# Priorities, smaller pieces and one step per visit in a kernel of four mixers

## The chip, the core and the metric

The kernel runs on one core of a Trainium2 chip. The time is that of the device for one execution, in microseconds. TensorE (PE) multiplies, VectorE (DVE), ScalarE (ACT) and GpSimd (POOL) do the rest, and SyncE (SP) issues the DMAs. Each engine works through a queue of its own that is written out when the program is built.

## The reference

One layer with four sequence mixers side by side, in fp32: x is 2048 tokens of 1024.

```python
h = rmsnorm(x, pre_norm_w)
p = h @ w_in                                  # 1024 -> 3992 columns
y_gdn  = gated_deltanet(p_gdn)                # conv, l2norm, chunks of 64, triangular solve, state 64x64 per head
y_rwkv = rwkv7(p_rwkv)                        # token shift, decay, delta rule with a learned rate, group norm, bonus
y_sc   = bg * causal_conv(cg * xv) * silu(z)  # short convolution
y_gla  = gla(p_gla)                           # gated linear attention, key width 32, value width 64
out = x + rmsnorm(concat(y_gdn, y_rwkv, y_sc, y_gla) @ w_out)
```

Each of the three recurrent mixers has 4 heads of 64 values. In gla, with q, k, v cut in chunks of 64 tokens and b the running sum of the log decay: `attn = tril((q e^b)(k e^-b)^T)`, `o = attn v + (q e^b) S`, `S = S e^(b_last) + (k e^(b_last - b))^T v`.

## The kernel before

The sequence is worked in four blocks of 512 tokens (`BL`), a block in four tiles of 128 (`TT`), a tile in two chunks of 64. Projections multiply in single-pass fp32 with each operand split in a high and a low part: three products per pair, so one projection tile of 128 columns is 24 matmuls of 512 tokens into one PSUM bank of two (`pp`). Weights are loaded per block (`load_parts`, in halves of 256 KB of columns; the split form comes from DRAM from the second block on).

The program is emitted by generators that are woven together (`weave`). The last one, the projections and then the output projection, is the main thread with number 99. Above it run the recurrences: `chains` (priority 0: state updates of gdn, rwkv and gla, tile by tile), `inverses` (1: the triangular inverses, two tiles of four heads at a time, by doubling in half precision), `prepare` (2: gates, norms, decays and matrices of both mixers), `put` and `rwkv_bonus` (3), the norms of the next block (4). A thread yields either an event that it waits for or a time (`LAT`) after which it may go on; the planner's clock `t` runs by the matmuls emitted. Whenever some thread is ready and the main thread has had `BEAT` = 1.5 of that clock, the ready threads are run, again and again until none is ready; then the main thread has the word again.

The order of emission is the priority of each instruction. `tc.high_priority(offset=n)` moves what is emitted in it n places ahead. The framework that builds the program lays out each engine's queue from these priorities and its own model of when an instruction can start. The evacuations of the projection banks have an offset of 400, as the weight splits have; everything in the mixers has none.

What the change touches: `inverse` (L591 to L658: copies to the block diagonal Bb and Yb, L613 W, L618 X, L620 the transpose Y), `gdn_chain` (L1005 to L1030, gu, the state Sg), `add_state` (L1037), `rwkv_chain` (L1056 ru, L1064 UV, L1079 the copy that ends a tile), `rwkv_prep` (two halves `pr` of 128 channels; scan L893, products L903 to L911), `gla_proj`, `proj_v`, `gla_prep`, and `gla` (L1286 to L1314). In gla's projection v is made by token: the normed input is the stationary operand and 256 weight columns move, into both banks at once, four quarters of the weights after another. One tile of `lv` then holds two tiles of tokens with 256 channels each. q, k and z are made by channel.

Of the kernel before, what the change touches and what calls it, by code (L numbers as in the profile page):

```python
# [19 lines left out]
P = 128  # L20
# [25 lines left out]
CST = {"ident": 0, "dlt": 128, "cum": 256, "msi": 384, "rst": 640, "bones": 640 + BL}  # L46
NCST = 640 + BL


def make_consts():  # L50
    c = np.zeros((P, NCST + P), np.float32)
    r = np.arange(P)
    blk = r[:, None] // 64 == r[None, :] // 64
    a, b = r[:, None] % 64, r[None, :] % 64
    c[:, 0:128] = np.eye(P)
    c[:, 128:256] = blk & (a > b)
    c[:, 256:384] = blk & (a <= b)
    j, i = r[:, None] % 64, np.arange(64)[None, :]

    c[:, 384:640] = np.concatenate([i > j, i >= j, i >= j, i > j], 1)  # L60
    c[:, 640:NCST] = np.arange(BL) % 64 > 0
    c[:, NCST:] = blk

    m = [j == i, -((j // 2 == i // 2) & (i % 2 == 1) & (j % 2 == 0)).astype(np.float32)]
    m += [-((j // (2 * s) == i // (2 * s)) & (j % (2 * s) >= s) & (i % (2 * s) < s)).astype(np.float32) for s in LEVELS]
    return c, np.concatenate([x.astype(np.float16) for x in m], 1)


def layout(inp):
# [4 lines left out]
    starts += [GLA0, GLA0 + 128, GLA0 + 512, GLA0 + 640]  # L74
# [5 lines left out]
    wv = w[:, GLA0 + 256:GLA0 + 512].reshape(KT, P, 256).transpose(1, 0, 2).reshape(P, KT * 256)  # L80
# [8 lines left out]
    for nm, key in (("w0", "rwkv_w0"), ("a0", "rwkv_a0"), ("kk", "rwkv_k_k"), ("ka", "rwkv_k_a"), ("rk", "rwkv_r_k"),  # L89
# [13 lines left out]
        "wv": wv,  # L103
# [24 lines left out]
class Ring:  # L128
# [6 lines left out]
    def __call__(self):  # L135
# [15 lines left out]
    "lqk": (BL, 2), "lv": (BL, 2), "lk": (128, 1), "lgz": (2 * BL, 1), "ld": (8, 1), "lg": (BL, 2), "n32": (32, 4), "gs": (TT, 2),  # L151
# [16 lines left out]

BEAT = 1.5
# [4 lines left out]
       "invr": 0.8, "chA": 1.0, "chB": 0.7, "chC": 0.48, "rpre": 5.0, "rchan": 4.5, "gpre": 3.0, "gA": 1.1,  # L174
# [14 lines left out]

class K:  # L190
    def __init__(self, tc, a, out):
        self.tc, self.nc, self.a, self.out = tc, tc.nc, a, out
        self.t, self.left, self.ev, self.threads = 0.0, 0.0, {}, []
# [11 lines left out]
    def thread(self, gen, prio):  # L205
        self.threads.append([prio, 0.0, None, gen])
        self.threads.sort(key=lambda th: th[0])
# [11 lines left out]
    def step(self, th):  # L219

        y = next(th[3], "end")
        if y == "end":
            self.threads.remove(th)
        elif isinstance(y, tuple):
            th[2] = y
        else:
            th[1] = self.t + y

    def weave(self):
# [3 lines left out]
        while self.threads:  # L233
            main = self.threads[-1]
            ready = [th for th in self.threads if th[0] < 99 and self.can(th)]
            if main[0] == 99 and self.can(main) and (not ready or self.t - self.left < BEAT):
                self.step(main)
            elif ready:
                while ready:
                    for th in ready:  # L240
                        self.step(th)
                    ready = [th for th in self.threads if th[0] < 99 and self.can(th)]
                self.left = self.t
            else:
                if not any(self.can(th) for th in self.threads):
                    w = [th[1] for th in self.threads if th[2] is None]
                    assert w, [(th[0], th[2]) for th in self.threads]
                    self.t = max(self.t, min(w))


    def setup(self, ctx):
# [29 lines left out]
        self.rst = g("rst", BL)  # L281
        c16 = c.tile([P, 64 * (2 + len(LEVELS))], F16, name="c16")
# [187 lines left out]
    def load_half(self, blk, wi, i):  # L470
# [10 lines left out]
    def proj(self, blk, groups):  # L481
# [3 lines left out]
        for n, (_, tiles, _) in enumerate(groups):  # L485
            nj = range(len(tiles))
            halves = [(n, j, i) for i in range(4 if tiles[0][0] == "v" else 2) for j in nj]
# [8 lines left out]
        for n, j, i, ks in work:  # L496
# [10 lines left out]
            if first:  # L507
                pss[n, j] = self.pp() if tiles[j][0] != "v" else [self.pp() for _ in range(2)]
# [3 lines left out]
            if tiles[j][0] == "v":  # L512
                yield from self.proj_v(ps, i, pairs)
                if i == 3:
                    with self.tc.high_priority(offset=PRIO):
                        tiles[j][1](ps)
                fin += 1
                continue
# [14 lines left out]
            yield 0.0  # L533

    def proj_v(self, ps, i, pairs):

        for q, (w, h) in enumerate(pairs):
            for k in range(2):
                for t in range(TT):
                    o = 256 * (t % 2)  # L540
                    self.mm(ps[t // 2][:, o:o + 256], h[:, 2 * i + k, t * P:(t + 1) * P], w[:, k, :], start=(i + q + k + t % 2 == 0),
                            stop=(i == 3 and q == 2 and k == 1), skip_group_check=True)
# [37 lines left out]
    def inverse(self, Bh, Bl, n):  # L580
# [9 lines left out]
        for c in range(2):  # L590
            nc.vector.tensor_copy(Bb[hs(c), :, hs(c)], Bh[hs(c)])  # L591
# [6 lines left out]
        nc.vector.tensor_tensor(Y, Bh, m4(self.n1t), ALU.mult)  # L598
        nc.vector.tensor_tensor(Y, Y, I16, ALU.add)
        X = self.R16["X"]()  # L600
        nc.vector.transpose(X, Y)
        def diag():
            Yb = self.Rbd["Yb"]()
            for c in range(2):
                nc.vector.tensor_copy(Yb[hs(c), :, hs(c)], Y[hs(c)])  # L605
# [3 lines left out]
        for lv in range(4):  # L609
# [3 lines left out]
            nc.vector.tensor_tensor(W, v(ps), m4(self.lev[lv]), ALU.mult)  # L613
# [4 lines left out]
            nc.vector.tensor_tensor(X2, v(ps), X, ALU.add)  # L618
            X = X2
            nc.vector.transpose(Y, X)  # L620
# [5 lines left out]
        nc.vector.tensor_tensor(W, v(ps), m4(self.lev[4]), ALU.mult)  # L626
# [8 lines left out]
        nc.vector.tensor_tensor(X2, v(px), X, ALU.add)  # L635
        nc.vector.tensor_tensor(Y, py, Y, ALU.add)
# [3 lines left out]
        nc.vector.tensor_tensor(T, I16, X, ALU.subtract)  # L640
# [8 lines left out]
        nc.vector.tensor_tensor(R, T, v(ps), ALU.subtract)  # L649
# [8 lines left out]
        nc.vector.tensor_tensor(v(Yf), v(ps), Y, ALU.add)  # L658
# [210 lines left out]
    def rwkv_prep(self, blk):  # L869
# [10 lines left out]
        for pr in range(2):  # L880
# [15 lines left out]
            nc.scalar.activation(e[:, :, 1:65], c3(G), AF.Exp)  # L896
            ev = e.rearrange("p (a c) t -> p a c t", c=2)
# [95 lines left out]
    def gdn_chain(self, tt, m, Y):  # L993
# [5 lines left out]
        for cp in range(2):  # L999
# [5 lines left out]
            nc.vector.tensor_tensor(h4(D)[q], h4(pA[:, 0:256])[q], bc(g["ne1"])[q], ALU.mult)  # L1005
            nc.vector.tensor_tensor(D[q], D[q], m["vT"][q], ALU.add)
            nc.vector.tensor_tensor(h4(t)[qn], h4(pA[:, 0:256])[qn], bc(g["e1s"])[qn], ALU.mult)
            n = 8 * cp + 2 * tt
            nc.vector.tensor_tensor(S, S, g["dec"][:, n:n + 2].unsqueeze(2).to_broadcast([P, 2, P]), ALU.mult)
# [5 lines left out]
            for hp in range(2):  # L1015
                nc.scalar.copy(qh(w)[q, :, hp, :], pB[hs(hp), 0:P].rearrange("p (q d) -> p q d", q=2))
# [12 lines left out]
        for cp in range(2):  # L1029
            nc.vector.tensor_tensor(og[hs(cp)], t[hs(1 - cp)], pO[hs(1 - cp), 0:256], ALU.add)  # L1030
        return og

    def add_state(self, S, pC):
        pv = pC[:, 0:P].rearrange("p (q d) -> p q d", q=2)
        for hp in range(2):
            sb = S[hs(hp), :, hs(hp)]
            self.nc.vector.tensor_tensor(sb, sb, pv[hs(hp)], ALU.add)  # L1037

    def rwkv_chain(self, tt, m, Y):
# [11 lines left out]
        for cp in range(2):  # L1051
# [4 lines left out]
            nc.scalar.copy(D[q], pAc[cp][q])  # L1056
            nc.vector.tensor_tensor(S, S, r["dec"][:, :, c:c + 1].to_broadcast([P, 2, P]), ALU.mult)
# [4 lines left out]
            for hp in range(2):  # L1062
                s = slice(4 * tt + hp, 4 * tt + hp + 3, 2)
                nc.vector.tensor_tensor(qh(uv[:, cp, :])[q, :, hp, :], pB[hs(hp), 0:P].rearrange("p (q d) -> p q d", q=2),  # L1064
# [13 lines left out]
        for cp in range(2):  # L1078
            nc.scalar.copy(og[hs(cp)], pAc[cp][hs(1 - cp)])  # L1079
# [156 lines left out]
    def gla_proj(self):  # L1236
# [4 lines left out]
        todo = [(None, ((WT_GLA + i, lambda ps, t=t: nc.scalar.copy(t, ps)),), None) for i, t in enumerate((qf, kf))]  # L1241
# [6 lines left out]
        todo.append((None, ((WT_GLA + 2, z(0)), (WT_GLA + 3, z(1))), "gla"))  # L1248
        return dict(q=qf, k=kf, v=v, gz=gz), todo

    def gla_prep(self):
# [24 lines left out]
    def gla(self, blk, tt):  # L1276
# [8 lines left out]
        at, ke, vt = u1(), self.R["lk"](), L["v"][tt // 2][:, 256 * (tt % 2):256 * (tt % 2) + 256]  # L1285
        nc.vector.tensor_tensor(h4(at), h4(pa[:, 0:256]), self.incl.unsqueeze(1).to_broadcast([P, 4, 64]), ALU.mult)  # L1286
        pt = self.psa()
        self.tr(pt[:, 0:P], L["ed"][:, ts], self.ident)
        nc.scalar.copy(ke, pt[:, 0:P])
# [7 lines left out]
        pC = pa[:, 256:320], pt[:, 128:192]  # L1297
# [4 lines left out]
        for cp in range(2):  # L1302
# [3 lines left out]
            nc.vector.scalar_tensor_tensor(self.Sl, self.Sl, L["dec"][:, c:c + 1], pC[cp], ALU.mult, ALU.add)  # L1306
# [7 lines left out]
        nc.scalar.copy(o, po[:, 0:256])  # L1314
# [145 lines left out]
```

## Time and profile before

| | |
|---|---|
| median of 3 runs | 1378.37 us (1376.46 to 1379.8) |
| the profiled execution | 1379.89 us, its span 1378.1 us |
| PE busy | 1284.7 us, 93%, 10088 matmuls |
| DVE / ACT / POOL busy | 967.7 / 530.2 / 355.5 us (70 / 38 / 26%) |
| granted clock of TensorE, mean | 0.985 |
| DMA | 204.63 MB, mean 148 GB/s |

The span cut in 40 equal slices; a digit is the busy share of a slice in tenths:

```
PE   5989988899999999999999999999998998999997
DVE  5766698869876895778657978888669847743232
```

[...] A wait is put down to the producer that came last.

### The profile page before, as it was taken

The numbers are of one execution on the slowest core, as the hardware profiler recorded it, in microseconds if no ns is written. First come the engines' busy times: TensorE is split into PE (matmuls) and PEld (weight loads), VectorE is DVE, ScalarE is ACT, GpSimd is POOL, SyncE is SP. The second block draws the span as 40 slices with busy tenths as digits, with TensorE's granted clock in tenths as the row PEclk, the third lists the DMA queues.
The fourth block names the chain that finished last, engine by engine and source line by source line (L and its number), as shares of the span: only waits on it lengthen the run. The fifth ranks groups of instructions, "written<-read, shape, count | busy, mean of one in ns | idle before, by whom it ended". The sixth has DMA issues, their size and how long they took to land. (4 is left out here: it accounts for less than half of the span.)

```text
span 1378.1 us, 26007 instructions
## 1 busy us (share of the span) xinstructions
PE 1284.7 (93%) x10088; PEld 982.1 (71%) x10088; DVE 967.7 (70%) x2194; ACT 530.2 (38%) x1167; POOL 355.5 (26%) x437
## 2 busy tenths in 40 slices
PE   5989988899999999999999999999998998999997
PEld 3767766767667767767777677776776776677886
DVE  5766698869876895778657977888669847743232
ACT  4663454336242431425423432453224325133221
POOL 5554444201221021101301210203111135233321
PEclk9999999999999999999999999999999999999999
DMA  8776554544244424453543335432444363233442
GB/s 283 263 258 231 206 177 146 177 152 133 82 139 146 157 89 135 146 177 105 173 146 130 130 120 174 144 110 68 127 143 145 103 198 121 89 99 116 151 151 100
DMA packets 98509, 204.63 MB, mean 148 GB/s; under 512 B 9153, under 2 KB 39249, under 8 KB 98385
## 3 DMA queue, kind: packets, MB, share of 16 engines
q1 hardware_dynamic: 98384, 202.96, 44.6%
q8 instruction: 79, 1.29, 0.4%
q14 instruction: 46, 0.37, 0.1%
HBM read 153.65 MB, written 49.28 MB: 147 GB/s over the span
## 5 line engine op out<-in xcount | busy, mean ns | idle before, releaser
L199 PE MATMUL pp<-hh,w 128*128 128x512 f32 (+1 forms) x2144 | 609.6, 408 | 7.6 <-DMA w<-parts 5.9
L199 PEld LDWEIGHTS pp<-hh,w 128*128 128x128 f32 (+1 forms) x2144 | 389.8, 190 | 92.0 <-issue 4.7
L199 PE MATMUL pp<-hl,w 128*128 128x512 f32 (+1 forms) x1088 | 323.1, 408 | 2.0 <-POOL hl L435 2.0
L199 PEld LDWEIGHTS pp<-hl,w 128*128 128x128 f32 (+1 forms) x1088 | 198.2, 190 | 45.4 <-POOL hl L435 3.8
L352 POOL TENSOR_TENSOR w<-raw,w 128x512 fp32r<-128x512 f32 (+1 forms) x102 | 129.3, 1270 | 223.6 <-ACT w L351 143.0
L351 ACT CAST w<-raw 128x512 fp32r<-128x512 f32 (+1 forms) x102 | 60.3, 593 | 130.5 <-issue 56.8
L356 POOL TENSOR_TENSOR sm<-sm,mhalf 128x4 f32<-128x4 f32 (+1 forms) x64 | 59.3, 927 | 193.4 <-DVE sm L1099 148.7
L199 PE MATMUL pp<-woh,w 128*128 128x512 f32 x256 | 71.8, 401 | 0.0
L681 DVE SCALAR_TENSOR_TENSOR pq<-pq,par,pq 128x512 f32<-128x512 f32 x72 | 59.4, 826 | 11.0 <-ACT pq L678 8.5
L605 DVE COPY Yb<-Y 64x512 f16<-64x512 f16 x160 | 55.8, 349 | 2.2
L199 PEld LDWEIGHTS <-Yb 128*128 128x128 f16 x640 | 25.2, 98 | 41.5 <-issue 22.9
L199 PEld LDWEIGHTS pp<-woh,w 128*128 128x128 f32 x256 | 47.6, 191 | 9.7
L199 PE MATMUL psi<-W,Yb 128*128 128x64 f16 x640 | 32.7, 194 | 22.3 <-DVE W L613 17.5
L618 DVE TENSOR_TENSOR X<-psi,X 128x512 f16<-128x512 f32 x64 | 43.9, 686 | 12.8 <-PE psi L199 12.5
L199 PEld LDWEIGHTS <-Bb 128*128 128x128 f16 x768 | 29.8, 99 | 29.5 <-issue 23.4
L613 DVE TENSOR_TENSOR W<-psi,c 128x512 f16<-128x512 f32 x64 | 43.8, 685 | 5.9 <-PE psi L199 5.3
L1393 DVE SCALAR_TENSOR_TENSOR pq<-pq,sm,x 128x512 f32<-128x512 f32 x32 | 24.6, 769 | 30.4 <-DMA x<-in_x 19.7
L620 DVE STREAM_TRANSPOSE Y<-X 128x512 f16<-128x512 f16 x64 | 45.2, 707 | 0.7
L199 PE MATMUL psi<-X,Bb 128*128 128x64 f16 x768 | 40.0, 195 | 6.2 <-DVE X L618 4.2
L1382 ACT ACTIVATE x<-pp 128x512 f32<-128x512 f32 x32 | 19.1, 598 | 64.1 <-PE pp L199 64.1
L847 ACT COPY pq<-pp 128x512 f32<-128x512 f32 x36 | 21.1, 586 | 53.0 <-PE pp L199 53.0
L199 PE MATMUL pp<-w,hh 128*128 128x256 f32 x256 | 36.6, 289 | 0.1
(320 smaller groups left out, 2152.4 us busy)
## 6 DMA issues: line engine op xcount, KB each, us to landing
w<-parts SPq DMA_DIRECT2D x174, 512.0 KB, 3.3
parts<-w SPq DMA_DIRECT2D x58, 512.0 KB, 4.0
raw<-in_wt SPq DMA_DIRECT2D x58, 256.0 KB, 3.2
x<-in_x SPq DMA_DIRECT2D x56, 256.0 KB, 3.0
raw<-yd SPq DMA_DIRECT2D x32, 256.0 KB, 2.9
out<-pq SPq DMA_DIRECT2D x32, 256.0 KB, 2.0
x<-in_xt SPq DMA_DIRECT2D x24, 256.0 KB, 2.9
w<-parts_v SPq DMA_DIRECT2D x12, 512.0 KB, 3.3
```

Source lines behind the costliest of these rows:

```text
L199: return self.nc.tensor.matmul(out, w, x, **kw)
L351: self.nc.scalar.copy(hi, src)
L352: self.nc.gpsimd.tensor_tensor(lo, src, hi.bitcast(F32), ALU.subtract)
L356: self.nc.gpsimd.tensor_tensor(dst, x, self.mhalf[:, 0:x.shape[1]], ALU.pow)
L605: nc.vector.tensor_copy(Yb[hs(c), :, hs(c)], Y[hs(c)])
L613: nc.vector.tensor_tensor(W, v(ps), m4(self.lev[lv]), ALU.mult)
L618: nc.vector.tensor_tensor(X2, v(ps), X, ALU.add)
L620: nc.vector.transpose(Y, X)
L681: nc.vector.scalar_tensor_tensor(acc, p[:, i:i + BL], self.pcol("conv", 4 * ct + i), acc, ALU.mult, ALU.add)
L847: nc.scalar.copy(p[:, 1:], ps)
L1382: nc.scalar.activation(junk, ps[i], AF.Square, accum_out=ss[:, i:i + 1])
L1393: nc.vector.scalar_tensor_tensor(o, o, r, x, ALU.mult, ALU.add)
```

## The change

It has four parts. First, a wrapper `Urgent` gives single operations an offset of 800: all VectorE and ScalarE operations of `inverse`, of both chains and of `add_state`, and those of `gla` up to its norm. `norm`, `gated`, the preparations and the matrices keep the plain calls. Second, `rwkv_prep` yields three times more in each half and its old yield falls from 5.0 to 1.0; `gla_prep` yields twice more. Third, a thread that has made a step and yielded a time above zero is not run again in the same visit of the weave. Fourth, v of gla is projected like all other tiles, by channel, 2 tiles of 128 channels, and each tile of tokens is transposed on TensorE beside the transpose of the decayed keys; one copy brings all three to SBUF. The mask `rst` of the scans moves to half precision.

```diff
+URGENT = 800
-       "invr": 0.8, "chA": 1.0, "chB": 0.7, "chC": 0.48, "rpre": 5.0, "rchan": 4.5, "gpre": 3.0, "gA": 1.1,
+       "invr": 0.8, "chA": 1.0, "chB": 0.7, "chC": 0.48, "rpre": 1.0, "burst": 0.5, "rchan": 4.5, "gpre": 3.0, "gA": 1.1,
+class Urgent:
+    def __init__(self, tc, eng):
+        self.tc, self.eng = tc, eng
+    def __getattr__(self, name):
+        op = getattr(self.eng, name)
+        def f(*a, **kw):
+            with self.tc.high_priority(offset=URGENT):
+                return op(*a, **kw)
+        return f
...
+        self.uv, self.ua = Urgent(tc, tc.nc.vector), Urgent(tc, tc.nc.scalar)
...
             th[1] = self.t + y
+            if y > 0.0:
+                th[4] = self.visit
...
             elif ready:
+                self.visit += 1
                 while ready:
                     for th in ready:
                         self.step(th)
-                    ready = [th for th in self.threads if th[0] < 99 and self.can(th)]
+                    ready = [th for th in self.threads if th[0] < 99 and self.can(th) and th[4] < self.visit]
...
-        self.rst = g("rst", BL)
+        c16 = c.tile([P, 64 * (2 + len(LEVELS)) + BL], F16, name="c16")
+        self.rst = c16[:, 64 * (2 + len(LEVELS)):]
...
-            nc.vector.tensor_tensor(W, v(ps), m4(self.lev[lv]), ALU.mult)
+            self.uv.tensor_tensor(W, v(ps), m4(self.lev[lv]), ALU.mult)
...
 rwkv_prep:
             nc.scalar.activation(e[:, :, 1:65], c3(G), AF.Exp)
+            yield LAT["burst"]
...
             nc.vector.tensor_tensor(slot(bks, 0), c4(ak), c4(en), ALU.mult)
+            yield LAT["burst"]
...
             nc.vector.scalar_tensor_tensor(m3(add[:, pr, :]), r_, self.pcol("rk", pr), k_, ALU.mult, ALU.mult)
+            yield LAT["burst"]
...
 gla_proj:
-        def fv(ps):
-            for t, p in zip(v, ps):
-                nc.scalar.copy(t, p)
-        todo.append((None, (("v", fv),), None))
+        todo = [(None, ((WT_GLA + i, lambda ps, t=t: nc.scalar.copy(t, ps)),), None) for i, t in enumerate([qf, kf] + v)]
...
 gla:
-        at, ke, vt = u1(), self.R["lk"](), L["v"][tt // 2][:, 256 * (tt % 2):256 * (tt % 2) + 256]
+        at, kv = u1(), self.R["lkv"]()
+        ke, vt = kv[:, 0:P], kv[:, P:]
...
-        self.tr(pt[:, 0:P], L["ed"][:, ts], self.ident)
-        nc.scalar.copy(ke, pt[:, 0:P])
+        for i, t in enumerate([L["ed"]] + L["v"]):
+            self.tr(pt[:, i * P:(i + 1) * P], t[:, ts], self.ident)
+        self.ua.copy(kv, pt[:, 0:3 * P])
```

The other replacements of `nc.vector` by `self.uv` and of `nc.scalar` by `self.ua` are of the same kind.

## Rows read from the trace of the kernel before

**Rows 1.** The page, busy us (share of the span) and instructions of each engine.

```profile
PE 1284.7 (93%) x10088; PEld 982.1 (71%) x10088; DVE 967.7 (70%) x2194; ACT 530.2 (38%) x1167; POOL 355.5 (26%) x437
```

**Rows 2.** Stretches: from:to, length, busy PE PEld DVE ACT POOL, PEclk, DMA, GB/s.

```profile
40.00:1240.00 1200.00, 1129.63 (x9341) 858.52 (x9339) 901.41 (x2060) 478.49 (x1050) 294.49 (x372) 0.98 0.45 146
170.00:215.00 45.00, 36.10 (x230) 27.38 (x229) 42.87 (x75) 22.23 (x39) 20.27 (x16) 0.92 0.52 178
...
1030.00:1075.00 45.00, 40.28 (x305) 30.16 (x303) 40.92 (x80) 21.81 (x39) 8.36 (x9) 1.00 0.43 142
```

**Rows 3.** Waits of PE: total us, times, longest us.

```profile
PE psi L199 <- DVE W L613: 17.5, 17, 4.8
...
PE psc L199 <- DVE gu L1006: 8.2, 16, 1.2
...
PE psa L199 <- DVE gk L728: 4.0, 3, 2.0
...
PE psa L199 <- DVE Y L636: 0.2, 1, 0.2
PE psa L203 <- ACT t L901: 0.2, 1, 0.2
```

**Rows 4.** Timeline of PE near 188 us: start, us, operation, [idle before, releaser].

```profile
187.88 0.58 PE L199 MATMUL psi<-W,Yb 128*128 128x64 f16 x8 [4.78 <-DVE W L613]
```

**Rows 5.** Timeline of DVE, 179 to 188 us.

```profile
179.82 1.15 DVE L909 TENSOR_TENSOR BK<-BK,t 128x512 f32<-128x512 f32 x1
180.89 1.78 DVE L910 TENSOR_TENSOR AR<-AR,E 128x512 f32<-128x512 f32 x1
182.60 2.77 DVE L605 COPY Yb<-Y 64x512 f16<-64x512 f16 x2
185.40 0.69 DVE L918 TENSOR_REDUCE n<-t 128x8 f32<-128x512 f32 x1
186.00 1.22 DVE L893 TENSOR_TENSOR_SCAN t<-cst,t 128x512 f32<-128x512 f32 x1
187.15 0.68 DVE L613 TENSOR_TENSOR W<-psi,c 128x512 f16<-128x512 f32 x1
```

**Rows 6.** Groups of PE by line and shape: count, busy us, mean ns, idle before.

```profile
L199 PE MATMUL pp<-w,hh 128*128 128x256 f32 x256 | 36.6, 289 | 0.1
...
L199 PE MATMUL pp<-w,hl 128*128 128x256 f32 x128 | 18.6, 288 | 0.0
...
L203 PE MATMUL psa<-cst,rv 128*128 128x128 f32 x32 | 7.0, 280 | 0.3 <-DVE M L964 0.3
```

**Rows 7.** Timeline of PE near 252 us, v of gla and what follows.

```profile
252.22 2.15 PE L199 MATMUL pp<-w,hh 128*128 128x256 f32 x16
254.31 0.27 PE L199 MATMUL psc<-gu,kT 64*64 64x64 f32 x2
```

**Rows 8.** Timeline of PE near 33 us, projections alone.

```profile
32.65 1.98 PE L199 MATMUL pp<-hh,w 128*128 128x512 f32 x8
34.46 1.07 PE L199 MATMUL pp<-hl,w 128*128 128x512 f32 x4
```

**Rows 9.** Timeline of PE near 64 us, four transposes and the next projections.

```profile
64.00 0.60 PE L203 MATMUL psa<-cst,kq 128*128 128x128 f32 x4
64.35 2.10 PE L199 MATMUL pp<-hh,w 128*128 128x512 f32 x8
```

**Rows 10.** Waits of DVE: total us, times, longest us.

```profile
DVE Sg L1037 <- PE psc L199: 20.3, 12, 2.6
...
DVE W L613 <- PE psi L199: 5.3, 8, 1.7
```

**Rows 11.** Timeline of ACT near 377 us, end of rwkv's chain of block 0.

```profile
377.51 0.74 ACT L1079 COPY or<-psc 64x256 f32<-64x256 f32 x2 [4.32 <-PE psc L199]
```

**Rows 12.** Timeline of DVE near 399 us, first AR of block 1.

```profile
399.48 0.75 DVE L852 SCALAR_TENSOR_TENSOR AR<-pq,par,pq 128x512 f32<-128x512 f32 x1 [1.19 <-ACT pq L848]
```

**Rows 13.** Group of ACT by line and shape: gla's copy of the keys.

```profile
L1289 ACT COPY lk<-psa 128x128 f32<-128x128 f32 x16 | 4.2, 263 | 6.4 <-PE psa L203 6.1
```

More of the change, by code (lines that the diff above doesn't have):

```diff
@@ L45 @@
 PAR, NPAR = _par_layout()
-CST = {"ident": 0, "dlt": 128, "cum": 256, "msi": 384, "rst": 640, "bones": 640 + BL}
-NCST = 640 + BL
+CST = {"ident": 0, "dlt": 128, "cum": 256, "msi": 384, "bones": 640}
+NCST = 640
 def make_consts():
@@ L73, in layout @@
     starts += [SC0 + P * i for i in range(8)]
-    starts += [GLA0, GLA0 + 128, GLA0 + 512, GLA0 + 640]
+    starts += [GLA0 + P * i for i in range(6)]
     tiles = [w[:, s:s + P].reshape(KT, P, P).transpose(1, 0, 2).reshape(P, KT * P) for s in starts]
@@ L102, in layout @@
         "wx": wx,
-        "wv": wv,
         "wo": wo.reshape(KT, P, D),
@@ L192, in __init__ @@
         self.tc, self.nc, self.a, self.out = tc, tc.nc, a, out
-        self.t, self.left, self.ev, self.threads = 0.0, 0.0, {}, []
+        self.uv, self.ua = Urgent(tc, tc.nc.vector), Urgent(tc, tc.nc.scalar)
+        self.t, self.left, self.visit, self.ev, self.threads = 0.0, 0.0, 0, {}, []
     def mm(self, out, w, x, **kw):
@@ L486, in proj @@
             nj = range(len(tiles))
-            halves = [(n, j, i) for i in range(4 if tiles[0][0] == "v" else 2) for j in nj]
+            halves = [(n, j, i) for i in range(2) for j in nj]
             order += halves
@@ L507, in proj @@
             if first:
-                pss[n, j] = self.pp() if tiles[j][0] != "v" else [self.pp() for _ in range(2)]
+                pss[n, j] = self.pp()
             if n == 0:
@@ L511, in proj @@
             ps, pairs = pss[n, j], loaded[at[n, j, i]]
[L512 to L518, printed above, removed]
             for q, (w, h) in enumerate(pairs):
@@ L532, in proj @@
                     self.done("P", blk, after, lat=2.5)
[L533 to L542, printed above, removed]
             yield 0.0
@@ L597, in inverse @@
         Y = self.R16["Y"]()
-        nc.vector.tensor_tensor(Y, Bh, m4(self.n1t), ALU.mult)
-        nc.vector.tensor_tensor(Y, Y, I16, ALU.add)
+        self.uv.tensor_tensor(Y, Bh, m4(self.n1t), ALU.mult)
+        self.uv.tensor_tensor(Y, Y, I16, ALU.add)
         X = self.R16["X"]()
-        nc.vector.transpose(X, Y)
+        self.uv.transpose(X, Y)
         def diag():
@@ L617, in inverse @@
             X2 = self.R16["X"]()
-            nc.vector.tensor_tensor(X2, v(ps), X, ALU.add)
+            self.uv.tensor_tensor(X2, v(ps), X, ALU.add)
             X = X2
-            nc.vector.transpose(Y, X)
+            self.uv.transpose(Y, X)
             Yb = diag()
@@ L634, in inverse @@
         X2 = self.R16["X"]()
-        nc.vector.tensor_tensor(X2, v(px), X, ALU.add)
-        nc.vector.tensor_tensor(Y, py, Y, ALU.add)
+        self.uv.tensor_tensor(X2, v(px), X, ALU.add)
+        self.uv.tensor_tensor(Y, py, Y, ALU.add)
         X = X2
         T = self.R16["X"]()
-        nc.vector.tensor_tensor(T, I16, X, ALU.subtract)
+        self.uv.tensor_tensor(T, I16, X, ALU.subtract)
         yield LAT["invr"]
@@ L657, in inverse @@
         Yf = self.R["Yf"]()
-        nc.vector.tensor_tensor(v(Yf), v(ps), Y, ALU.add)
+        self.uv.tensor_tensor(v(Yf), v(ps), Y, ALU.add)
         return v(Yf)
@@ L1015, in gdn_chain @@
             for hp in range(2):
-                nc.scalar.copy(qh(w)[q, :, hp, :], pB[hs(hp), 0:P].rearrange("p (q d) -> p q d", q=2))
+                self.ua.copy(qh(w)[q, :, hp, :], pB[hs(hp), 0:P].rearrange("p (q d) -> p q d", q=2))
             yield LAT["chB"]
@@ L1029, in gdn_chain @@
         for cp in range(2):
-            nc.vector.tensor_tensor(og[hs(cp)], t[hs(1 - cp)], pO[hs(1 - cp), 0:256], ALU.add)
+            self.uv.tensor_tensor(og[hs(cp)], t[hs(1 - cp)], pO[hs(1 - cp), 0:256], ALU.add)
         return og
@@ L1036, in add_state @@
             sb = S[hs(hp), :, hs(hp)]
-            self.nc.vector.tensor_tensor(sb, sb, pv[hs(hp)], ALU.add)
+            self.uv.tensor_tensor(sb, sb, pv[hs(hp)], ALU.add)
     def rwkv_chain(self, tt, m, Y):
@@ L1055, in rwkv_chain @@
                 self.mm(pAc[cp][:, P * pr:P * pr + P], r["AR"][pr][:, c, :], S[:, pr, :], start=False, stop=True, skip_group_check=True)
-            nc.scalar.copy(D[q], pAc[cp][q])
-            nc.vector.tensor_tensor(S, S, r["dec"][:, :, c:c + 1].to_broadcast([P, 2, P]), ALU.mult)
+            self.ua.copy(D[q], pAc[cp][q])
+            self.uv.tensor_tensor(S, S, r["dec"][:, :, c:c + 1].to_broadcast([P, 2, P]), ALU.mult)
             yield LAT["chB"]
@@ L1078, in rwkv_chain @@
         for cp in range(2):
-            nc.scalar.copy(og[hs(cp)], pAc[cp][hs(1 - cp)])
+            self.ua.copy(og[hs(cp)], pAc[cp][hs(1 - cp)])
         return og
@@ L1240, in gla_proj @@
         gz = self.R["lgz"]().rearrange("p (q t) -> p q t", q=2)
-        todo = [(None, ((WT_GLA + i, lambda ps, t=t: nc.scalar.copy(t, ps)),), None) for i, t in enumerate((qf, kf))]
-        def fv(ps):
-            for t, p in zip(v, ps):
-                nc.scalar.copy(t, p)
-        todo.append((None, (("v", fv),), None))
+        todo = [(None, ((WT_GLA + i, lambda ps, t=t: nc.scalar.copy(t, ps)),), None) for i, t in enumerate([qf, kf] + v)]
         z = lambda pr: lambda ps: self.gate(gz[:, pr, :], ps, self.d[:, 16:17])
-        todo.append((None, ((WT_GLA + 2, z(0)), (WT_GLA + 3, z(1))), "gla"))
+        todo.append((None, ((WT_GLA + 4, z(0)), (WT_GLA + 5, z(1))), "gla"))
         return dict(q=qf, k=kf, v=v, gz=gz), todo
@@ L1305, in gla @@
                 self.mm(po[hs(cp), hs(h)], self.qbd[:, cp, h, :], self.Sl, start=False, stop=True, skip_group_check=True)
-            nc.vector.scalar_tensor_tensor(self.Sl, self.Sl, L["dec"][:, c:c + 1], pC[cp], ALU.mult, ALU.add)
+            self.uv.scalar_tensor_tensor(self.Sl, self.Sl, L["dec"][:, c:c + 1], pC[cp], ALU.mult, ALU.add)
             if cp == 0:
@@ L1313, in gla @@
         o = u1()
-        nc.scalar.copy(o, po[:, 0:256])
+        self.ua.copy(o, po[:, 0:256])
         self.norm(o, u1, EPS, False)
```

35 lines of the change are left out of this document (16 added, 19 removed).

## The prediction

> **What bounds the kernel now.** I read the page's engine line first. TensorE has work in 93% of the span [rows 1], so only two things can shorten the run: less TensorE work, or fewer pauses and less half-speed time of TensorE. The stretches say where the pauses are: 1378.1 - 1284.7 = 93.4 us in all, and 1200 - 1129.6 = 70.4 us of it lies between 40 and 1240 us, while the mixers run [rows 2]. Before 40 us the kernel waits for its first inputs, and the last 100 us or so are output projections back to back (nines of the PE line of the slices); the change touches neither.
>
> Then the view of TensorE's waits. Sort its lines by whether the producer becomes urgent. Fifteen do (from W at L613, 17.5 us, through gu at L1006, 8.2 us, down to Y at L636, 0.2 us); they add up to 46.2 us. Eleven lie in the same stretch and don't become urgent (from gk at L728, 4.0 us, to t at L901, 0.2 us): 17.2 us [rows 3]. The rest is the start, weights coming by DMA, and gaps too short to be listed.
>
> Why does W come late? The longest single pause, 4.78 us before 187.88 us, is a second inverse product waiting for W [rows 4]. In VectorE's timeline just ahead of that W stand four operations of rwkv's preparation, L909 and L910 before the copies Yb and L918 and L893 behind them: 1.15 + 1.78 + 0.69 + 1.22 = 4.84 us, all on tiles that nothing in this inverse needs [rows 5]. So the pause is a matter of order in VectorE's queue. [...]
>
> **The change part by part.** Durations are from the profiled execution, 1379.9 us for a span of 1378.1; the median of the runs shown is 1378.4, so I take 1.5 us off at the end.
>
> *Priority.* Nothing is computed more or less; operations of the inverse, the chains and gla go ahead of other ready ones on VectorE and ScalarE. All of a wait goes if its cause is an operation like those of [rows 5] in front; none if the producer itself is too slow. Bounds: 0 and 46.2 us. The one wait I could take apart goes whole (4.84 against 4.78), so I take two thirds: -31 us. *One step per visit* helps the same waits: a thread's next step can't be emitted before the projections have had their 1.5 us, in practice eight matmuls of 512 columns, 34.46 - 32.65 = 1.81 us [rows 8]. A producer of 0.7 us that isn't queued behind others is covered by that. I count both edits in the one term. What is late next are the producers that don't get priority.
>
> *Pieces.* rwkv_prep and gla_prep issue the same instructions, broken by yields of 0.5; the planner's 5.0 behind each half of rwkv_prep shrinks to 1.0. The total of VectorE work in its four stretches stays. Its effect is already in the waits above, so no separate term; if a piece only comes later, the room is that of the next paragraph but one.
>
> *Clock.* At the 4.78 us pause the half-speed time costs (1 - 0.92) x 45 = 3.6 us [rows 2]. If the pause goes, so does this: -3.5 us. Other half-speed stretches I leave; bounds 0 and (1 - 0.98) x 1200 = 24 us [rows 2].
>
> *What is pushed back.* gates, norms, the matrices of gdn and rwkv and the gated outputs stay at their place and now stand behind urgent operations. Their eleven waits, 17.2 us [rows 3], could vanish with shorter queues or double: bounds -17 and +17. One urgent VectorE operation in front is about 0.7 us (W itself in [rows 5]), eleven lines with some twenty single waits; half of these lengthened by it is +6 us. The epilogues of the projections lose their place too. TensorE now never waits for them: no line of the waits names one. Each bank is filled by 24 matmuls, 24 x 0.227 = 5.4 us by [rows 8], while the other bank is emptied. The cover is this 5.4 us; if it were gone, each of some 116 projection tiles could wait 0.7 us, 81 us. Bounds 0 and 81; nearest to the row that shows no such wait I take +3.
>
> *gla's v by channel.* Taken away: 384 matmuls of 256 columns; added: 192 of 512 and 32 transposes of 128 x 128. Undisturbed, 16 of the narrow ones take 254.31 - 252.22 = 2.09 us [rows 7], 0.131 each, 50.2 us; 192 wide ones at 0.2265 [rows 8] are 43.5. That saves 6.7. A transpose is 0.35 / 4 = 0.088 us between neighbours [rows 9] or 7.0 / 32 = 0.22 by its group's busy time [rows 6]: +2.8 to +7.0, and I take 4.0, nearer to the streak since they come three in a row. By busy time alone the old v costs 36.6 + 18.6 = 55.2 us [rows 6], more than the streak, since it too is broken up. Net -2.7, bounds -4 and +3. The bigger copy on ScalarE (384 columns for 128) costs at least nothing and at most two further copies of 0.263 us each [rows 13], 16 x 0.53 = 8.4 us of an engine that is 38% busy [rows 1], and no wait of TensorE names L1289; I count zero, and up to 8 us if gla's chain were what the end waits for. v's copies out of the two banks stay eight of the same size. Weight transfers: four halves of 256 KB per block before and after, in the same queue.
>
> [...]
>
> *The mask in half precision.* 12 scans read it; the eight of rwkv take 1.22 us each, as the one in [rows 5]. Bounds: the same, or half. Both lie on VectorE outside an urgent path: zero.
>
> Sum: -31 - 3.5 + 6 + 3 - 2.7 = -28 us; 1379.9 - 28.2 = 1351.7 in the profile, about **1350** in the median.
>
> [...]
>
> **The rivals.**
> *A. The waits change place.* The preparations and epilogues pushed back cost what the chains win: +17 and +14 in place of +6 and +3. For it: VectorE is full in the preparation stretches [rows 2], where someone must be late. Against: outside of these it has a quarter of its time free (901 of 1200 us busy). 1350 + 22 = 1372, between 1366 and 1385.
> *B. Slower: an urgent operation holds the queue.* Place: VectorE. It already stands still for TensorE's results of the chains, in nine lines from Sg (20.3 us, 12 times) to W (5.3 us, 8 times) [rows 10], together 118 us. An operation put further ahead waits longer there, and an epilogue or preparation that could run stands behind it. If these waits grow by half (59 us) and two thirds of it reach TensorE, 39 us, while half of the gain stays: 1378.4 - 14 + 39 = 1403. It decides from the point at which new waits of TensorE for epilogues exceed 28 us. For it: those 118 us are there. Against: the queue's order comes from a schedule in which a later producer is also seen as later. [...]
> *C. The chains fall behind.* rwkv's last pair of a block has 12 steps; with one per visit it can be late by 12 x 1.81 = 22 us. The copy that ends it is at 377.5 us and the first overwrite of its tile AR by the next block at 399.5 [rows 11, 12]: 22 us of room. Beyond that each microsecond stops the projections, at three hand-overs; 10 us each: 1350 + 30 = 1380.
> *D. Nearly all goes.* All 46.2 us, 12 us of clock, 4 of v, nothing pushed back: 1378.4 - 62 = 1316, up to 1335 with a third of it missing.
>
> **How the numbers follow.** The forecast (1335 to 1366) 0.49, A 0.13, B 0.16 (1385 to 1420), C 0.06 (1375 to 1395), D 0.16 (1310 to 1335). Under 0.2%, 2.8 us, this kernel's measurement can't tell from no change. Faster: 0.49 + 0.16 + 0.05 of A = 0.70. Same: 0.06 of A and 0.02 of C = 0.08. Slower: 0.16 + 0.04 of C + 0.02 of A = 0.22. The range 1322 to 1398 leaves out about half of D and half of B.
>
> **What would show it.** Right: W and gu together far below their 25.7 us [rows 3]; no half-speed stretch at the first rwkv preparation; TensorE's idle between 40 and 1240 us near 45 instead of 70 us; 384 narrow matmuls gone. Wrong: new lines in TensorE's waits for ACT or DVE at pp, or the eleven lines without priority above 30 us in place of 17.2 (A, B); projections without work at a hand-over (C).

## The result and the profile after

The changed kernel takes 1383.48 us in the median of 20 runs (1378.69 to 1391.42), the one before 1378.17 us in 20 runs beside it (1370.01 to 1381.35): a ratio of 1.0051, 95% interval 1.0038 to 1.0065. It is slower by 5 us between the medians and by 7 by the ratio, where 28 us less were forecast. The profiled execution of the changed kernel happens to be the shortest of its 20, 1378.69 us for a span of 1376.9 us. Its views show where the forecast gain stayed out; they can't show the 5 to 7 us.

The page of the changed kernel, its engine line, beside [rows 1]:

```profile
PE 1281.5 (93%) x9928; PEld 968.9 (70%) x9928; DVE 975.8 (71%) x2194; ACT 531.3 (39%) x1165; POOL 355.7 (26%) x437
```

TensorE's busy time fell by 3.2 us, its pauses rose from 93.4 to 1376.9 - 1281.5 = 95.4 us. The stretches of the changed kernel, columns as in [rows 2]:

```profile
40.00:1240.00 1200.00, 1128.85 (x9195) 846.88 (x9195) 911.04 (x2063) 480.42 (x1051) 295.84 (x373) 0.98 0.44 147
170.00:215.00 45.00, 37.95 (x218) 28.24 (x217) 37.47 (x65) 21.90 (x37) 23.04 (x18) 0.91 0.54 184
240.00:285.00 45.00, 40.60 (x374) 30.58 (x372) 37.16 (x79) 14.85 (x32) 14.11 (x13) 0.96 0.46 157
```

Between 40 and 1240 us TensorE stands still for 71.2 us, as before (70.4); 45 were forecast. The granted clock at the first rwkv preparation (170 to 215 us) is 0.91, not better than 0.92. TensorE's waits in the changed kernel (total us, times, longest); operations with priority all bear the wrapper's line L201:

```profile
PE psc L215 <- DVE gu L201: 18.4, 19, 2.3
PE psi L215 <- DVE W L201: 12.3, 21, 1.6
...
PE psi L215 <- DVE X L201: 4.7, 6, 1.7
...
PE psc L215 <- ACT ru L201: 3.0, 3, 1.6
PE psc L215 <- DVE UV L201: 3.0, 6, 0.8
PE pp L215 <- ACT pq L561: 3.0, 2, 2.5
PE psa L215 <- POOL S L372: 3.0, 1, 3.0
...
PE pp L215 <- DVE lg L670: 1.6, 2, 0.9
```

Under the wrapper's line three lines that write W fall together. Two of them stand beside the 17.5 us of L613 in the kernel before:

```profile
PE psi L199 <- DVE W L626: 2.1, 3, 1.0
PE psi L199 <- DVE W L649: 0.8, 1, 0.8
```

So, against [rows 3], W went from 20.4 to 12.3 us and its longest wait from 4.8 to 1.6, gu went from 8.2 to 18.4, and epilogues (pq, lg), which no wait named before in this stretch, stop the projections for 4.6 us. Summed over all lines that got priority the waits are 46.3 us before and 46.7 after; over the others between 40 and 1240 us that don't stand at a projection, 17.1 and 19.0.

The pause of [rows 4] did shrink. TensorE of the changed kernel at the same product:

```profile
188.88 0.41 PE L215 MATMUL psi<-X,Bb 128*128 128x64 f16 x8
189.12 2.09 PE L215 MATMUL pp<-hh,w 128*128 128x512 f32 x8
192.64 0.39 PE L215 MATMUL psi<-W,Yb 128*128 128x64 f16 x8 [1.43 <-DVE W L201]
```

Its VectorE and its GpSimd meanwhile:

```profile
189.42 0.70 DVE L201 STREAM_TRANSPOSE Y<-X 128x512 f16<-128x512 f16 x1
190.05 0.70 DVE L910 SCALAR_TENSOR_TENSOR radd<-AR,par,BK 128x512 f32<-128x512 f32 x1
190.68 0.58 DVE L201 COPY Yb<-Y 64x512 f16<-64x512 f16 x2
191.29 0.69 DVE L912 TENSOR_TENSOR BK<-BK,t 128x512 f32<-128x512 f32 x1
191.90 0.68 DVE L201 TENSOR_TENSOR W<-psi,c 128x512 f16<-128x512 f32 x1
189.39 0.19 POOL L1222 COPY pq<-halo_s 128x2 f32<-128x2 f32 x1 [0.44 <-DMA yd<-pq]
191.49 1.62 POOL L372 TENSOR_TENSOR S<-radd,S 128x512 fp32r<-128x512 f32 x1 [1.91 <-ACT S L371]
```

Two things stand here that the forecast didn't have. Two operations of rwkv's preparation (L910, L912) still go ahead of W, though W is urgent and the product that it reads ended at 189.29 us. And the two copies Yb take 0.58 us in place of 2.77 [rows 5], with GpSimd idle beside them: 2.2 of the 3.35 us by which this pause shrank. The last section returns to that.

Other pauses are new. TensorE of the changed kernel near 246 us:

```profile
241.74 0.28 PE L215 MATMUL psc<-Sg,kq 128*128 128x128 f32 x1
241.78 2.07 PE L215 MATMUL pp<-hh,w 128*128 128x512 f32 x8
246.19 0.45 PE L215 MATMUL psc<-gu,Yf 64*64 64x64 f32 x8 [2.34 <-DVE gu L201]
```

and its VectorE meanwhile:

```profile
242.84 0.42 DVE L201 TENSOR_TENSOR gu<-psc,gk 64x256 f32<-64x256 f32 x1
243.29 1.35 DVE L201 TENSOR_TENSOR Sg<-Sg,sx 128x256 f32<-128x256 f32 x1
244.67 0.42 DVE L201 TENSOR_TENSOR gu<-psc,sx 64x256 f32<-64x256 f32 x1
245.12 0.93 DVE L201 TENSOR_TENSOR gu<-gu,vT 64x256 f32<-64x256 f32 x1
```

What TensorE waits for is the last of the four. The state decay `Sg` (L1009 of the kernel before) stands ahead of it, since it is urgent as well and its input is there earlier. Counted over the trace, it stands there in 28 of 32 steps, and in none before the change. That order alone doesn't make the 18.4 us: with priority alone (b_urgent below) the decay stands there in 30 of 32 steps, and the waits on gu are 7.8 us. In this pause `Sg` and the last `gu` also took 1.35 and 0.93 us in place of 0.42 each, 1.4 of the 2.34 us (last section).

### The profile page after: what moved, and what is told of

It reads as the page before. It is cut to its first block, busy times and chain, and to the rows that moved or that the text cites. A ratio compares the mean times of both kernels' runs of the same rounds, so it can differ in the third digit from the quotient of the medians.

```text
span 1376.9 us, 25685 instructions
## 1 busy us (share of the span) xinstructions
PE 1281.5 (93%) x9928; PEld 968.9 (70%) x9928; DVE 975.8 (71%) x2194; ACT 531.3 (39%) x1165; POOL 355.7 (26%) x437
## 5 line engine op out<-in xcount | busy, mean ns | idle before, releaser
L215 PE MATMUL pp<-hh,w 128*128 128x512 f32 (+1 forms) x2272 | 639.0, 407 | 7.0 <-ACT pq L561 3.0
L215 PEld LDWEIGHTS pp<-hh,w 128*128 128x128 f32 (+1 forms) x2272 | 411.7, 190 | 97.5 <-issue 8.9
L215 PE MATMUL pp<-hl,w 128*128 128x512 f32 (+1 forms) x1152 | 338.4, 408 | 2.0 <-POOL hl L455 2.0
L215 PEld LDWEIGHTS pp<-hl,w 128*128 128x128 f32 (+1 forms) x1152 | 209.2, 189 | 47.7 <-POOL hl L455 3.8
L201 DVE TENSOR_TENSOR W<-psi,c 128x512 f16<-128x512 f32 x80 | 54.5, 682 | 9.1 <-PE psi L215 8.2
L201 DVE TENSOR_TENSOR X<-psi,X 128x512 f16<-128x512 f32 x80 | 54.7, 684 | 8.8 <-PE psi L215 8.4
L201 DVE COPY Yb<-Y 64x512 f16<-64x512 f16 x160 | 52.2, 326 | 1.8
L215 PEld LDWEIGHTS <-Yb 128*128 128x128 f16 x640 | 24.8, 98 | 33.3 <-issue 18.7
L201 DVE STREAM_TRANSPOSE Y<-X 128x512 f16<-128x512 f16 x64 | 45.1, 704 | 0.6
L201 ACT COPY gu<-psc 64x128 f32<-64x128 f32 x64 | 16.7, 260 | 58.6 <-PE psc L215 52.0
```

The lines of the kernel that those rows point to most:

```text
L201: return op(*a, **kw)
L215: return self.nc.tensor.matmul(out, w, x, **kw)
```

## The experiments

All ratios are to the kernel before, run on the same chip between the others, with 95% intervals; the groups of runs are from four chips. Names with b_ are edits of the kernel before, names with a_ edits of the changed kernel. Waits and pauses are from one profiled execution of each. Theories: the waits of the chains are what the time hangs on, and one part of the change moves them (which?); against it, that any new order of the queues moves the time by half a per cent either way, whatever was meant by the edit (S in the last group of expectations; in the first group and for a_gu, S means that the state's decay ahead of gu is what costs).

**Which part.** b_urgent has the wrapper and its calls, b_visit the rule of one step per visit, b_v gla's projection by channel (each with the mask in half precision); a_plain is the changed kernel without priority.

```diff
 b_urgent
+        self.uv, self.ua = Urgent(tc, tc.nc.vector), Urgent(tc, tc.nc.scalar)
...
 b_visit
-  ready = [... self.can(th)]
+  ready = [... self.can(th) and th[4] < self.visit]
 b_v
-  starts += [GLA0, GLA0 + 128, GLA0 + 512, GLA0 + 640]
+  starts += [GLA0 + P * i for i in range(6)]
...
 a_plain
-        self.uv, self.ua = Urgent(tc, tc.nc.vector), Urgent(tc, tc.nc.scalar)
+        self.uv, self.ua = tc.nc.vector, tc.nc.scalar
```

> The kernel before with the priority of 800 alone (and the half-precision mask). My theory F (TensorE's queue follows the faster producer): W comes sooner after its product (1.7 us instead of 2.36 us, as in the changed kernel), but the matmul that uses it is drawn nearer in the queue as well, so TensorE's waits on urgent lines stay at 40 to 50 us and the time at 1374 to 1384 us. Theory S (the state's decay is now ahead of gu): waits on gu rise from 8 to about 18 us, time 1383 to 1390. The forecast's theory: waits fall to about 15 us, time near 1350.

> The kernel before with one step per visit alone (and the half-precision mask). Theory D (the rule delays the chains and buys nothing): gdn's chain of block 0 ends at 265 to 275 us instead of 256 and the time is 1380 to 1388. The forecast's theory: a step always has 1.8 us of projections before it, waits on the mixers' products fall by 10 us or more, time 1360 to 1370.

> The kernel before with v of gla by channel alone (and the half-precision mask). By the rows of before: TensorE's work falls by 2.7 us (between -4 and +3), time 1375 to 1376. If the streak of narrow matmuls was no slower per column in practice, or the transposes stand in the way of gla's chain: 1378 to 1382.

> The changed kernel without the priority of 800. Theory F: 1380 to 1386, no change against 1383.5, waits of TensorE on the mixers' products 40 to 50 us. Theory S: the 10 us of waits on gu go away, 1371 to 1376. The forecast's theory (priority was worth 31 us, something else cost 36): 1400 or more.

Measured: b_urgent 1.0022 (1.0002 to 1.0042), b_visit 1.0006 (0.9984 to 1.0028), b_v 1.0002 (0.9983 to 1.0022), a_plain 1.0046 (1.0026 to 1.0065). No part alone gains, and without priority the changed kernel is as slow as with it. TensorE's waits in b_urgent between 40 and 1240 us:

```profile
PE psi L217 <- DVE W L203: 10.5, 18, 2.8
PE psc L217 <- DVE gu L203: 7.8, 13, 1.2
PE psi L217 <- DVE X L203: 6.7, 9, 1.9
PE psa L221 <- DVE or L1125: 5.9, 4, 2.6
PE psc L217 <- DVE Sg L203: 4.3, 5, 2.1
PE psa L217 <- DVE t L823: 3.9, 1, 3.9
PE psa L221 <- ACT t L923: 3.9, 4, 2.0
PE psa L217 <- POOL S L374: 3.8, 3, 2.2
PE psa L221 <- ACT BK L997: 2.6, 4, 1.4
```

Priority alone shortens the waits of its own lines from 46.3 to 34.6 us, 12 of the 31 forecast. The lines without it (in the view or, t twice, S, BK) grow from 17.1 to 24.8 us and take 8 of the 12 back. The pair of a_plain and the changed kernel, which differ in the priority alone, says the same: 53.6 and 46.7 us on the lines with priority, 9.8 and 19.0 on the others. Of the theories for b_urgent, the forecast's (waits about 15 us, time near 1350) and S (gu at 18 us) fell; F has the time right, but its waits of 40 to 50 us are too long.

**The waits taken away.** b_free lets the two inverse products read a constant mask in place of W, and gdn's product read vT in place of gu, so their operands are never late; that part of the result is not computed. Beside it stand the pieces alone, the changed kernel with whole preparations, and the changed kernel without the visit rule.

```diff
 b_free
-            mmb(ps, Yb, W)
+            for u in range(U):
+                self.mm(v(ps)[:, u, :], Yb[:, u, :], self.n1t, start=True, stop=True)
...
-  self.mm(pB[hs(h % 2), hs(h // 2)], Y[q, h, :], D[q, hs(h)], start=True, stop=True)
+  self.mm(pB[hs(h % 2), hs(h // 2)], Y[q, h, :], m["vT"][q, hs(h)], start=True, stop=True)
 b_pieces (a_whole is the reverse on the changed kernel)
-  "rpre": 5.0
+  "rpre": 1.0, "burst": 0.5
+            yield LAT["burst"]   # five places
 a_anyvisit
-  ready = [... self.can(th) and th[4] < self.visit]
+  ready = [... self.can(th)]
```

> The kernel before; the inverse's second product reads a constant mask instead of W, and gdn's second product reads vT instead of D, so TensorE has nothing to wait for at W (17.5 + 2.1 us of waits) and at gu (8.2 us); the results of both are left out of the computation. If TensorE's waits are worth their length, as the forecast took them: 1378 - 28 = 1350. If a wait that goes is taken over by the next one in the chain (theory M, the chains' latency is what is waited for): 1365 to 1376.

> The kernel before with the pieces of both preparations alone (5.0 becomes 1.0, five yields of 0.5). From the first four runs: visits, v and pieces together cost 0.46% (1380.1), visits and v alone nothing. If the pieces are the cause (theory P): 1379 to 1383. If only the combination is: 1373 to 1378.

> The changed kernel with the preparations whole again (yield 5.0). Theory P: about 1377, the changed kernel's loss gone but for the priority's 3 us. If pieces cost nothing: 1381 to 1385.

> The changed kernel without the rule of one step per visit. If the rule delays the first block's gdn chain (270 us against 256) and that costs: 1376 to 1379, end of this chain back at 256 to 260 us. If the rule buys cover for the products: 1386 to 1395.

Measured: b_free 0.9955 (0.9939 to 0.9971), b_pieces 0.9901 (0.9879 to 0.9923), a_whole 0.9996 (0.9981 to 1.0012), a_anyvisit 0.9899 (0.9876 to 0.9923). b_free did only half of what it was for. The pause for W is still there, 4.77 us for 4.78, though the product no longer reads W. TensorE in b_free:

```profile
189.59 0.58 PE L199 MATMUL psi<-c,Yb 128*128 128x64 f16 x8 [4.77 <-DVE W L613]
```

The inverse has one PSUM bank (`"psi": 1` in `BANKS`), and W is what empties it: the next product waits for the bank as well as for the operand. Only gu's 8.2 us went. The time fell by 6.2 us, into the range of theory M (1365 to 1376). Its profile agrees with M: TensorE's pauses are 92.6 us in place of 93.4, so other lines took over nearly all of the 8.2, and the span is shorter mostly by busy time (1281.0 us for 1284.7, with a granted clock of 0.988 for 0.985). But a difference of 0.45% alone proves neither theory, as the next runs show. The pieces gain 1% on the kernel before, and putting the preparations back whole gains 0.55% on the changed one: opposite signs for one edit.

**How much does any edit move?** b_rpre1 and b_rpre45 change one number of the planner and nothing else. a_prepfree exempts the preparations from the visit rule; a_gu takes the priority from the two operations that stand in front of gu.

```diff
 b_rpre1 (b_rpre45)
-  "rpre": 5.0
+  "rpre": 1.0 (4.5)
 a_prepfree
-  ... and th[4] < self.visit]
+  ... and (th[0] == 2 or th[4] < self.visit)]
 a_gu
-  self.uv.tensor_tensor(h4(t)[qn], h4(pA[:, 0:256])[qn], ...)
+  nc.vector.tensor_tensor(h4(t)[qn], h4(pA[:, 0:256])[qn], ...)
...
-  self.uv.tensor_tensor(S, S, g["dec"]..., ALU.mult)
+  nc.vector.tensor_tensor(S, S, g["dec"]..., ALU.mult)
```

> The kernel before with the one number of rwkv_prep's yield changed, 5.0 to 1.0, and no further yields. Theory Y (the long yield held the preparation back): all of the pieces' gain comes from it, 1364 to 1368. Theory B (the breaks let projections in between VectorE's bursts): no gain, 1374 to 1380.

> The kernel before with the same number at 4.5 instead of 5.0, an edit without a meaning for the kernel that still changes the queues' order. Theory L (the order of the queues is so sensitive that any such edit moves the time by 0.5 to 1%): outside 1375 to 1380. Theories Y and B: 1375 to 1380.

> The changed kernel with the rule of one step per visit for all threads but the preparations. Theory V (under the rule each added yield costs the preparation a visit of at least 1.8 us): the pieces' gain comes back, 1364 to 1372. If the rule costs through the chains' or inverses' steps: 1379 to 1386.

> The changed kernel with two of gdn's operations without priority, t (L1007) and the state's decay (L1009), so that the sum gu (L1006) is again the first after its product. Theory S: TensorE's waits on gu fall from 18 to about 8 us and the time by as much, 1373 to 1376. Since the waits on W and gu were worth a fifth of their length in the kernel before: 2 us of time, 1380 to 1383.

Measured: b_rpre1 1.0062 (1.0040 to 1.0084), b_rpre45 0.9942 (0.9920 to 0.9963), a_prepfree 1.0026 (1.0011 to 1.0041), a_gu 0.9989 (0.9976 to 1.0003). A number moved from 5.0 to 4.5 is worth as much as the whole change, with the other sign. b_rpre1 is slower than both of its theories said, and a_prepfree (1378.3 us) lies outside the ranges of both of its own. a_gu does about half of what it was to do to gu's wait: from 18.4 to 13.0 us, where 8 were expected. TensorE's waits in a_gu:

```profile
PE psi L215 <- DVE W L201: 14.2, 23, 1.7
PE psc L215 <- DVE gu L201: 13.0, 16, 1.7
```

and it is 0.6% faster than the changed kernel, but a step of that size could come from the new order alone.

**Pairs in another order.** The same two moves of numbers that mean nothing for the change, on the kernels whose differences were in question.

```diff
 b_out7, a_out7, a_any_out7 (on a_anyvisit), b_pieces_out7 (on b_pieces)
-  "out": 8.0
+  "out": 7.0
 b_mats, a_mats
-  "mats": 2.2
+  "mats": 1.7
```

> The kernel before with one number of the planner's table moved, "out" 8.0 to 7.0: nothing is computed otherwise, only the order of the queues changes. Theory S (any new order of the queues moves the time, whatever it was meant to do): a ratio anywhere between 0.990 and 1.006, since the two moves of 5.0 gave 0.9942 and 1.0062. Theory C (the change itself costs 0.5%): this is before again, 1.000 within 0.002.

> The changed kernel with the same move, "out" 8.0 to 7.0. Theory C: 0.5% above b_out7 as the changed kernel is above before, so 1.005 if b_out7 is 1.000. Theory S: between 0.990 and 1.006 again, and its distance from b_out7 need not be +0.5%; a distance below 0 or above 0.9% speaks for S.

> The changed kernel without the rule of one step per visit and with "out" 8.0 to 7.0. Theory V (the rule itself costs 1%, since without it the changed kernel took 0.9899 instead of 1.0051): 1.0 to 1.5% below a_out7, near 0.990. Theory S: between 0.990 and 1.006, within 0.6% of a_out7 on either side.

> The kernel before with another number of the table moved, "mats" 2.2 to 1.7. Theory S: between 0.990 and 1.006, and not the same as b_out7 (over 0.3% apart). Theory C: 1.000 within 0.002.

> The changed kernel with "mats" 2.2 to 1.7, the second pair beside b_mats (0.9996). Theory C (the change costs 0.5% in any order of the queues): 1.005. Theory S (the scatter of the order): between 0.990 and 1.006; below 1.002 speaks against C, since then two of two moves took the difference away.

> The preparations in pieces alone, on the kernel before, with "out" 8.0 to 7.0. Theory P (the pieces themselves gain 1%, as they did with 8.0): 0.990, or 0.987 if the move's own 0.3% in b_out7 adds to it; below 0.993 speaks for P. Theory S: between 0.990 and 1.006, and closer to 1.000 than 0.990 was; above 0.996 speaks for S.

| numbers of the planner | before | changed | changed, no visit rule | before with pieces |
|---|---|---|---|---|
| as they were | 1.0000 | 1.0051 (1.0038 to 1.0065) | 0.9899 (0.9876 to 0.9923) | 0.9901 (0.9879 to 0.9923) |
| "out" 7.0 | 0.9970 (0.9950 to 0.9990) | 0.9974 (0.9953 to 0.9995) | 1.0017 (0.9995 to 1.0038) | 0.9998 (0.9980 to 1.0016) |
| "mats" 1.7 | 0.9996 (0.9976 to 1.0016) | 1.0020 (1.0005 to 1.0035) | | |

The change costs 0.51%, 0.04% and 0.24% in the three rows. The rule of one step per visit costs 1.5% in the first row and gains 0.4% in the second. The 1% of the pieces is gone in the second. So the two large effects, of the visit rule and of the pieces, did not outlast a new order of the queues, and the slowing of the change itself is between nothing and 0.5%: three pairs with a mean of 0.26% don't tell it from zero. A gain of 2% is excluded in each of them. Five orders of the kernel before (the column and the two moves of "rpre") lie between 0.9942 and 1.0062, three of the changed one between 0.9974 and 1.0051. One rival stays open: b_pieces and a_anyvisit ran on another chip than b_pieces_out7 and a_any_out7, and no kernel but the one before was measured on two chips. The two moves of "rpre", 1.2% apart, ran on one and the same chip, so the scatter itself is not one of chips.

Part of what differs between such orders is how long TensorE pauses. Engine lines of the page, the pieces alone with a span of 1366.8 us:

```profile
PE 1283.0 (94%) x10088; PEld 984.4 (72%) x10088; DVE 955.6 (70%) x2194; ACT 529.2 (39%) x1165; POOL 359.7 (26%) x437
```

and a_any_out7 with 1374.2 us:

```profile
PE 1274.3 (93%) x9928; PEld 964.5 (70%) x9928; DVE 977.1 (71%) x2194; ACT 531.9 (39%) x1165; POOL 352.1 (26%) x437
```

That is 83.8 and 99.9 us of pauses. Over the 20 kernels the pauses of the one profiled execution and the measured ratio have a correlation of 0.62, and a microsecond of pause goes with about one of time. The rest is not in the pauses. The slowest kernel, b_rpre1 (a span of 1383.8 us), pauses 94.0 us, hardly more than the kernel before with 93.4; its TensorE is busy for 5.1 us longer, at a granted clock of 0.980 for 0.985:

```profile
PE 1289.8 (93%) x10088; PEld 985.6 (71%) x10088; DVE 969.9 (70%) x2194; ACT 527.8 (38%) x1165; POOL 359.1 (26%) x437
```

In a_any_out7 the largest waits are, between 40 and 1240 us,

```profile
PE psi L215 <- DVE W L201: 17.9, 21, 3.1
PE psc L215 <- DVE gu L201: 12.2, 16, 3.4
PE psa L219 <- DVE or L1106: 6.2, 5, 3.5
```

and in a_anyvisit, 1.2% faster, the same W and gu are shorter:

```profile
PE psi L215 <- DVE W L201: 13.7, 21, 3.7
PE psc L215 <- DVE gu L201: 10.3, 14, 3.4
```

The same waits are longer or shorter in another order; what stands beside them in each was not followed up.

The fastest versions run, b_pieces and a_anyvisit, beat both kernels by 1.0 and 1.5%. As far as these runs go they are good orders that were found, not better rules: with "out" at 7.0 the same kernels stand at 0.9998 and 1.0017.

## Why the prediction was wrong

*The step that failed* is the first term, "All of a wait goes if its cause is an operation like those of [rows 5] in front", and from it -31 us. Part of the cause was read rightly: with priority W comes earlier. From the end of the product that feeds it to the end of W it takes 2.36 us before, 1.54 in b_urgent and 1.70 in the changed kernel (2.24 without priority, in a_plain; mean of all). But the step failed in three places, and of the 31 us none came: the lines with priority wait for 46.7 us after 46.3.

First, operations like those of [rows 5] are still in front. Between the product's end and W, VectorE spends 1.07 us on operations without priority in the kernel before, 0.39 in b_urgent and 0.49 in the changed kernel (0.89 in a_plain). And the one wait that was taken apart, 4.84 against 4.78 us, was misread: 2.2 us of it were the copies Yb at five times their own length (2.77 us for the two, 0.58 in the changed kernel).

Second, the urgent operations stand in each other's way. From the end of its product to the end of the last gu it takes 2.20 us before and 2.58 in b_urgent, 2.33 in a_plain and 2.69 in the changed kernel: for the second-largest wait the producer came later, not earlier. With the priority taken from two of the urgent operations that stood ahead of it, a_gu, it is 2.11.

Third, what was taken as fixed, the order of TensorE, isn't. Between the product psi<-X,Bb and the next one that needs W, TensorE has on average 9.6 projection matmuls in the kernel before, 8.2 in b_urgent and 7.4 in the changed kernel (8.3 in a_plain). 2.2 matmuls of 0.227 us from start to start [rows 8] (the page gives each 0.408 us of busy time, which overlaps the next) are 0.5 us of cover given up for 0.66 us of lead. With 8 or fewer of them to cover W stand 55 of 80 products before and 77 after. The likely reason is that the program that lays out the queues sees the producer earlier and puts the consumer earlier; the traces show the order, not the reason. So waits remain, in part on other lines, and what the lines with priority win in b_urgent and against a_plain (12 and 7 us) the lines without it lose (8 and 9). That is rival A in kind (1366 to 1385 us). Its place differs when the whole change is compared with the kernel before: there the waits moved chiefly from W to gu, inside the urgent lines.

*One step per visit* was to add to the same gain. Alone it is 1.0006, with W's cover unchanged (9.5 matmuls).

*Clock*, -3.5 us: nothing. In the kernel before the granted clock is 0.50 from 185.4 to 192.2 us, beside the pause that ends at 187.88, and 1.00 from 170 to 185 us. In the changed kernel that pause shrank to 1.43 us and the clock is 1.00 from 188 to 205 us, but it is 0.66 from 175 to 180, 0.75 from 205 to 215 and 0.69 from 246 to 250 us (0.96 between 240 and 285 us, where it was 1.00 before), and the mean is 0.985 in both kernels. That the slow time goes with the pause was an estimate and no run shows it: the pause of 2.09 us that ends at 211.03 us in the kernel before has a clock of 1.00 around it (205 to 220 us).

*Pushed back*, +6: right in kind, +8 in b_urgent and +9 against a_plain; against the kernel before only +2, since the other edits had shortened these waits. *Epilogues*, +3: 4.6 us of waits at pp, of the size forecast; the 5.9 us that the kernel before waited there for weights fell to 0.8.

*v by channel*, -2.7: TensorE's busy time is 5.9 us lower in b_v (1278.8 for 1284.7) and the time the same (-2.3 to +3.0 us by its interval). The pauses grew by 2.4 us in its profile. *The mask*: the zero was right. The scans of the changed kernel, mean 1214 ns against 1215:

```profile
L893 DVE TENSOR_TENSOR_SCAN t<-c,t 128x512 f32<-128x512 f16 x8 | 9.7, 1214 | 2.6 <-ACT t L891 2.5
```

*Pieces* without a term: 0.9901 alone, but 0.9998 in another order, so zero was not shown wrong.

*The rivals.* B fell: VectorE's waits for results of the chains, 118 us in [rows 10] and the lines like them, are 112 us after, with two more lines of W and X (5 us before) among them that share the wrapper's line. C fell too: rwkv's chain of block 0 ends at 380.1 us in place of 378.3, and the first overwrite of AR comes at 403.17 in place of 399.48 [rows 11, 12], so the room stayed. ScalarE of the changed kernel at the end of that chain:

```profile
379.35 0.75 ACT L201 COPY or<-psc 64x256 f32<-64x256 f32 x2 [0.39 <-PE psc L215]
```

D had the failed step in full. What no rival held is the scatter between orders: it is some ±0.6%, 8 us, larger than every term of the sum but the first, and the chances should have had it.

## What to carry to other kernels

Where a scheduler lays out the queues, an operation that becomes urgent can pull its consumer with it: count the work that covers the wait on the consumer's engine, not only how late the producer is. Before a difference of half a per cent is given a cause, move a number that means nothing, on both kernels, and see whether the difference stays. And look at which buffer the waiting instruction writes, not only at what it reads.

## What was not expected of the hardware

In both traces many of VectorE's operations with all operands in SBUF take up to several times as long while GpSimd works. In the changed kernel `Sg<-Sg,sx` takes 0.42 us on average (at most 0.43) in the 22 cases with GpSimd idle, and 0.86 (up to 1.50) in the 10 with it at work; the copies Yb 0.28 and 0.48 (up to 1.39), five times as long at most. Transposes (`Y<-X`, 0.703 us in 24 cases beside GpSimd, 0.705 in the others) and reductions (`n<-t`, 0.670 us in 7 cases, 0.681 in the others) keep their length. Operations of the same size that read PSUM don't change either: `gu<-psc,gk` 0.42 us in both, W 0.68 in both. GpSimd of the kernel before, during the copies Yb of [rows 5] (182.60 to 185.37 us):

```profile
182.08 1.73 POOL L352 TENSOR_TENSOR S<-radd,S 128x512 fp32r<-128x512 f32 x1
183.76 0.24 POOL L1219 COPY pq<-halo_s 128x2 f32<-128x2 f32 x1
183.96 1.25 POOL L352 TENSOR_TENSOR w<-raw,w 128x512 fp32r<-128x512 f32 x1
```

So two copies of 0.28 us took 2.77. The prediction had no row of GpSimd for this pause. In all, VectorE's operations beside GpSimd's are some 70 us longer than alone before the change and some 74 after. Of TensorE's waits for VectorE, 23 of 60 us before and 21 of 56 after have an operation in them that is lengthened by more than 0.1 us. No run took the GpSimd work away, so that this is the cause is read from the overlap and not tested.
